# Another order in the opening of a two-layer decoder trunk, transposes where float32 blocks were multiplied with the identity, and casts of the sums of h put in turn with the attention's

## The chip, the cores and the metric

The kernel runs on one core of one Trainium2 chip. The metric is device microseconds of one execution. A core has TensorE (PE in the profile; its weight loads are PEld), VectorE (DVE), ScalarE (ACT), GpSimd (POOL) and SyncE (SP), whose queue issues the DMAs.

## The reference

Two layers, each a token mixer and a gated convolutional FFN, on x of 1024 tokens by 1024 features, all in float32:

```python
for l in range(DEPTH):                       # 2
    h = rmsnorm(x, norm1[l])
    proj = h @ w_in[l]                       # 1024 x 5120: q/k/v of both mixers, two gates
    qa, ka, va, qb, kb, vb, gate_pre = jnp.split(proj, splits, axis=-1)
    o_a = dilated_mixture(...)               # 3 groups of 4 heads, windows 128/512/2048, dilations 1/4/16
    o_b = stick_breaking_attention(...)      # 4 heads
    gates = jax.nn.sigmoid(gate_pre + b_gate[l])
    merged = g_a * (o_a @ w_br[l, :OUT_A]) + g_b * (o_b @ w_br[l, OUT_A:])
    x = x + merged @ w_o[l]
    up = rmsnorm(x, norm2[l]) @ w_up[l]      # 1024 x 5632
    a, v = up[..., :D_FF], up[..., D_FF:]
    a = causal_depthwise_conv(a, conv_w[l], conv_b[l])
    x = x + (jax.nn.gelu(a, approximate=False) * v) @ w_down[l]
return rmsnorm(x, norm_f)
```

## The kernel before

Activations lie with features on the partitions and tokens along the free axis, in two halves of 512 tokens (`n` = 0, 1). Every large operand of a product is kept in two parts: `split` (L124) has ScalarE cast the source to a high part (line L125) and VectorE subtract it for the low part (L126). A product is then three matmuls: high by high, high by low, low by high (`product`, L147; lines L151 to L153). Small products that need full float32, such as a product with the identity matrix `ident`, are issued as one float32 matmul.

TensorE's order is the order of the program text (`manual_schedule`). The orders of ScalarE, VectorE, GpSimd and of SyncE's queue are made by the compiler's scheduler from dependencies, priorities and modelled costs, and are fixed when the program runs: an instruction that waits holds up what stands behind it on its engine. Buffers are allocated from pools by tag; an allocation waits until a buffer of its tag is free (tag `e8` has 6, `xa` 4, `p4` 4, `ql` 2, `wh` and `wl` 4 each; PSUM has two banks for each of the tags `ps`, `s`, `t` and `o`).

**The opening.** `first` (L1761) brings x in, 128 tokens (a chunk) at a time: DMA of 512 KB, square and root on ScalarE (L1778, L1779), a reciprocal (L1780) and two multiplications with the gain (L1783) on VectorE, eight transposes (L1786, tile `x_t`) on TensorE, and a two-part cast into H (tiles `hh` and `hl`). `mixer` (L1114) issues the attention's masks (`masks`, L79), starts the small loads of `setup` (L1792), and then lets `drive` alternate: one chunk of `first`, two steps of `head` (L559). `head` loads and casts the weights for the stick-breaking mixer's values, keys and queries, and computes the values of one chunk (`values_part`, L494, two steps of 12 matmuls each, tile `v_ps`), then keys and queries.

**The attention and what runs beside it.** `attend` (L307) goes through a list of items: stick-breaking (B..), near window (N.., `p0` tiles) and dilated windows (T.., `p1` tiles). Between two operations of an item it advances the dense work by a rate, some matmuls of the gates, further projections and so on. An item transposes its weights to PSUM, `parts` (L583) casts them in two (tiles `p0h`, `p0l`) with high priority, and `apply` multiplies them with the values (L709). Each call of `advance` first calls `aside` (L224), which takes one step from a list of side work. The list begins with `block_sums` (L889): four sums of blocks of H for the products that are done with seven block products instead of eight (`seven`). The first two series of sums (numbers 3 and 1) take three GpSimd subtractions or additions for each of four blocks (L900 to L902, tile `h_sum`), and then `in_two` (L914) casts each in two (tiles `t_hi`, `t_lo`). In `series` (L920) a sum begins every `gap` = 5 steps, and its cast comes `lag` = 4 steps after it. Series 3 begins after item B17, series 1 after the scores of N01.

**Products with the identity.** `join` (L852) ends a pair of heads: it spreads 16 blocks of factors (`fx`, 128x128) by multiplying them with `ident` (L860, tile `j_ps`), into two banks of `t` and two of `o`; the bank of `o` that is used last is released by `fold` (L596), which takes the attention's last output out of it. `norm` (L455) spreads the reciprocal roots of four blocks of tokens in the same way (L470, tile `nrm_b`). `join` runs four times, `norm` six.

**The residual.** Near the end of layer 0's mixer `residual_in` (L1100) loads x again, a chunk at a time, turns it (tile `x_t`, L1111), and ScalarE copies it to the residual stream X (L1112).

## Time and profile before

| | |
|---|---|
| median of 3 runs | 2724.53 us (2723.65 to 2727.9) |
| the profiled execution | 2726.66 us |
| its span in the trace | 2724.8 us |
| instructions | 36820 |
| TensorE busy | 2678.4 us, 98% of the span |
| VectorE, ScalarE, GpSimd busy | 74%, 50%, 25% |
| mean granted clock of TensorE | 0.996 |
| DMA | 420.52 MB, mean 154 GB/s |

The span is the time from the first to the last recorded instruction; the execution's time lies a little over it. A row of a timeline gives the start, the duration, engine, line, operation, tiles written and read, how many instructions are merged in it, and in brackets how long the engine had stood idle before it and what ended that. In a row of a stretch the numbers after the length are busy us (and instructions) of PE, PEld, DVE, ACT and POOL, then TensorE's granted clock, the DMA engines' busy share and GB/s. A matmul's recorded duration overlaps the next one's; the distance of two starts is what it costs.

### The profile page before, as it was taken

What the parts mean: (1) busy time and instruction counts of PE and PEld (TensorE: products, weight loads), DVE (VectorE), ACT (ScalarE), POOL (GpSimd) and SP (SyncE); (2) the same over time, 40 slices, a digit from 0 to 9 for tenths busy, and PEclk for the clock granted to TensorE, in tenths of its full rate; (3) what the DMA queues carried; (4) which work ended last, traced back from release to release, by engine and by line L of the source; (5) the groups of instructions that cost most, each with busy time, mean ns of one, the idle gap of its engine ahead of it and who ended that gap; (6) DMA issues with size and microseconds to landing.
All of it is one profiled execution on the core that took longest, in us unless ns stands there. A gap on an engine that the chain in (4) does not pass through costs nothing.

```text
span 2724.8 us, 36820 instructions
## 1 busy us (share of the span) xinstructions
PE 2678.4 (98%) x13194; PEld 2249.0 (83%) x13194; DVE 2018.9 (74%) x2976; ACT 1352.2 (50%) x2494; POOL 669.0 (25%) x485
## 2 busy tenths in 40 slices
PE   8999999999999999999999999999999999999999
PEld 8987888888888888888888878888788888888888
DVE  5776766675789888897657767565848888998865
ACT  5655545465455555432335556454645455554225
POOL 1004211122124433321110051211212343443210
PEclk9999999999999999999999999999999999999999
DMA  5112268564334444688411122784722444446863
GB/s 152 34 53 69 60 173 260 176 225 130 89 116 164 139 161 139 216 325 315 165 36 42 48 82 61 198 257 162 257 87 81 141 152 149 170 139 245 330 252 123
DMA packets 356738, 420.52 MB, mean 154 GB/s; under 512 B 20700, under 2 KB 285260, under 8 KB 355020
## 3 DMA queue, kind: packets, MB, share of 16 engines
q1 hardware_dynamic: 356556, 418.18, 46.4%
q8 instruction: 104, 1.70, 0.3%
q14 instruction: 78, 0.64, 0.1%
HBM read 278.59 MB, written 139.53 MB: 153 GB/s over the span
## 4 chain that ended last, share of the span: by engine, by line
PE 83%; DVE 9%; issue 2%; ACT 2%; POOL 2%; DMA 1%; SPq 0%; DVEq 0%; ACTq 0%; POOLq 0%
PE u_a L883 5%; PE u_a L885 5%; PE u_a L884 5%; PE d_ps L1585 4%; PE d_ps L1586 4%; PE d_ps L1587 4%; PE u_c L885 3%; PE u_c L883 3%; PE u_c L884 3%; PE i_a L883 2%; PE i_a L884 2%; PE i_a L885 2%; PE o_ps L151 2%; PE o_ps L152 2%; PE o_ps L153 2%
## 5 line engine op out<-in xcount | busy, mean ns | idle before, releaser
L126 DVE TENSOR_TENSOR w_lo<-up_a,w_hi 128x512 fp32r<-128x512 f32 x240 | 237.4, 996 | 21.9 <-ACT w_hi L125 21.9
L125 ACT CAST w_hi<-up_a 128x512 fp32r<-128x512 f32 x240 | 149.4, 622 | 185.2 <-PE u_a L884 43.2
L1593 DVE TENSOR_TENSOR x<-x,d_ps 128x512 f32<-128x512 f32 (+1 forms) x228 | 151.8, 671 | 78.1 <-PE d_ps L1587 76.6
L1324 POOL TENSOR_TENSOR cv<-cv 128x512 f32<-128x512 f32 x88 | 132.3, 1516 | 249.3 <-DVE cv L1319 139.5
L126 DVE TENSOR_TENSOR w_lo<-w_raw,w_hi 128x512 fp32r<-128x512 f32 x152 | 112.6, 743 | 60.7 <-ACT w_hi L125 60.3
L126 DVE TENSOR_TENSOR g<-cv,g 128x512 fp32r<-128x512 f32 x154 | 152.5, 991 | 5.2 <-ACT g L125 2.7
L125 ACT CAST w_hi<-w_raw 128x512 fp32r<-128x512 f32 x152 | 94.2, 620 | 114.9 <-PE o_ps L152 71.2
L126 DVE TENSOR_TENSOR w_lo<-in_a,w_hi 128x512 fp32r<-128x512 f32 x120 | 87.9, 734 | 67.5 <-ACT w_hi L125 66.9
L125 ACT CAST w_hi<-in_a 128x512 fp32r<-128x512 f32 x120 | 74.5, 621 | 122.2 <-PE i_c L884 49.4
L1585 PE MATMUL d_ps<-gd_in,w_hi 128*128 128x512 f32 (+1 forms) x340 | 130.3, 383 | 1.7 <-issue 0.8
L1587 PE MATMUL d_ps<-gd_in,w_lo 128*128 128x512 f32 (+1 forms) x340 | 129.8, 382 | 0.0
L1586 PE MATMUL d_ps<-gd_in,w_hi 128*128 128x512 f32 (+1 forms) x340 | 129.8, 382 | 0.0
L883 PE MATMUL u_a<-hh,w_hi 128*128 128x512 f32 x320 | 124.6, 390 | 2.1 <-DVE u L1475 2.1
L884 PE MATMUL u_a<-t_lo,w_hi 128*128 128x512 f32 x320 | 124.5, 389 | 0.0
L883 PE MATMUL u_a<-t_hi,w_hi 128*128 128x512 f32 x320 | 124.5, 389 | 0.0
L884 PE MATMUL u_a<-hl,w_hi 128*128 128x512 f32 x320 | 124.5, 389 | 0.0
L885 PE MATMUL u_a<-hh,w_lo 128*128 128x512 f32 x320 | 124.5, 389 | 0.0
L885 PE MATMUL u_a<-t_hi,w_lo 128*128 128x512 f32 x320 | 124.5, 389 | 0.0
L623 DVE TENSOR_TENSOR_SCAN stay<-stay,zero 128x128 f32<-128x128 f32 (+3 forms) x64 | 86.9, 1357 | 42.7 <-ACT stay L621 42.5
L1585 PE MATMUL d_ps<-gd_in,wd 128*128 128x512 f32 (+1 forms) x292 | 113.9, 390 | 0.0
L125 ACT CAST g<-cv 128x512 fp32r<-128x512 f32 x154 | 94.9, 616 | 37.5 <-POOL cv L1324 29.8
L1587 PE MATMUL d_ps<-gd_in,wd 128*128 128x512 f32 (+1 forms) x292 | 112.8, 386 | 0.0
(398 smaller groups left out, 8659.0 us busy)
## 6 DMA issues: line engine op xcount, KB each, us to landing
gd<-g SPq DMA_DIRECT2D x154, 512.0 KB, 3.4
gd_in<-gd SPq DMA_DIRECT2D x154, 512.0 KB, 6.4
up_a<-in_w_up_dram SPq DMA_DIRECT2D x80, 512.0 KB, 5.6
t_kq<-tk SPq DMA_DIRECT2D x32, 768.0 KB, 4.9
wd_raw<-in_w_down_dram SPq DMA_DIRECT2D x22, 1024.0 KB, 8.5
w_raw<-in_w_in_dram SPq DMA_DIRECT2D x80, 256.0 KB, 3.1
in_a<-in_w_in_dram SPq DMA_DIRECT2D x40, 512.0 KB, 4.6
gin<-gs SPq DMA_DIRECT2D x32, 512.0 KB, 4.7
```

Source lines behind the costliest of these rows:

```text
L125: act.copy(hi, src)
L126: dve.tensor_tensor(lo, src, f32(hi), ALU.subtract)
L151: pe.matmul(o, lh, rh, start=(first and i == 0), stop=False, skip_group_check=share)
L623: dve.tensor_tensor_scan(rev, rev, zero[:, 0:1].to_broadcast([P, L]), 1.0, ALU.mult, ALU.add)
L883: pe.matmul(o, w[0][:, c], rh, start=(first and i == 0), stop=False, skip_group_check=True)
L884: pe.matmul(o, w[0][:, c], rl, start=False, stop=False, skip_group_check=True)
L885: pe.matmul(o, w[1][:, c], rh, start=False, stop=(last and i == 3), skip_group_check=True)
L1324: return lambda: pool.tensor_tensor(dst, a, b, ALU.subtract)
L1585: pe.matmul(o[:, sub], wh[:, c], gh[:, sub], start=(i == 0 and k in (0, 4, 5)), stop=False, skip_group_check=True)
L1586: pe.matmul(o[:, sub], wh[:, c], gl[:, sub], start=False, stop=False, skip_group_check=True)
L1587: pe.matmul(o[:, sub], wl[:, c], gh[:, sub], start=False, stop=(i == m - 1), skip_group_check=True)
L1593: dve.tensor_tensor(x, x, o[:, sub], ALU.add)
```

## The change

1. The opening is written out in another order. x's first chunk is also transposed as it came (`kept`), stored to DRAM later and reloaded into X, so that `residual_in` leaves that chunk out. The value weights are loaded and cast by `first` itself, two of their four low parts on GpSimd; their loads stand behind those of x's first two chunks. One warming matmul less is issued. The squares go to tag `e8` instead of `ql`. Casts of chunk i follow the scaling of chunk i+1. `mixer` issues the first three chunks with ScalarE and VectorE in the order of the text: a chunk, one step of values, a chunk, one step, the masks, a chunk, two steps. The loads of key and query weights and of `setup` come later.
2. `norm` and `join` use a transpose in place of the float32 matmul with `ident`.
3. In `block_sums` the GpSimd operations are chained one sum after the other; a sum's ScalarE cast is ordered after the last attention cast that was issued before it (an ordering alone, no wait); the gap is 4 steps instead of 5, and the lag 6 instead of 4.

```diff
--- before.py
+++ after.py
@@ -31,10 +31,11 @@
 GRP = 2
 NRAW = 2
 PT = 6
-WARM = 6
+WARM = 5
 GROUPS = (2, 2, 3, 4)
 READY = 6
 ET = mybir.EngineType
+NO_SYNC = mybir.DependencyInfo(mybir.DependencyClass.NoSync, mybir.DependencyReason.DATA)
 IN_ORDER = {ET.PE, ET.Activation, ET.DVE, ET.Pool}
 HEAD = 4
 SECOND = 0.35
@@ -121,8 +122,16 @@
     def quarter(name, dtype=F32, c=HF):
         return sb.tile([P, 2048 // c, c], dtype, tag="xa", bufs=4, name=name)
 
-    def split(hi, lo, src):
-        act.copy(hi, src)
+    LAST = {}
+
+    def split(hi, lo, src, turn=None):
+
+
+        one = act.copy(hi, src)
+        if turn == "is":
+            LAST["act"] = one.ins.name
+        elif turn == "waits" and LAST:
+            tc.add_manual_dep(one.ins, LAST["act"], NO_SYNC, reason="in turn")
         dve.tensor_tensor(lo, src, f32(hi), ALU.subtract)
 
 
@@ -467,7 +476,7 @@
         yield
         rb = bank(tag, "nrm_b")
         for c in range(4):
-            pe.matmul(rb[:, c * P : (c + 1) * P], ss[:, 4 + c : 5 + c].to_broadcast([P, P]), ident, start=True, stop=True, skip_group_check=True)
+            pe.transpose(rb[:, c * P : (c + 1) * P], ss[:, 4 + c : 5 + c].to_broadcast([P, P]), ident)
         yield
         new_h(n)
         for e in range(KD):
@@ -563,13 +572,20 @@
             x = [big(name, F32R) for _ in range(n)] if l else None
             return x and ([x[0][:, h, :] for h in range(2)] if n == 1 else [y.rearrange("p a b -> p (a b)") for y in x])
 
-        wv = weights(w_in[l][:, OFF_VB : OFF_VB + 256], 256, place(2, "v_w"))
-        wk, wq = (weights(w_in[l][:, off : off + P], P, place(1, "kq_w")) for off in (OFF_KB, OFF_QB))
+        wv = weights(w_in[l][:, OFF_VB : OFF_VB + 256], 256, place(2, "v_w")) if l else early.pop("wv")
+        others = lambda: [weights(w_in[l][:, off : off + P], P, place(1, "kq_w")) for off in (OFF_KB, OFF_QB)]
+        if l:
+            wk, wq = others()
         yield
         vt = R["vb"] = new_v("vb")
         kt = R["kb", 0] = big("kt", F32R)
         q = R["qb", 0] = new_q()
-        yield from values_part(vt, wv, range(2 if l else 4))
+        if l:
+            yield from values_part(vt, wv, range(2))
+        else:
+            yield from values_part(vt, wv, range(1))
+            wk, wq = others()
+            yield from values_part(vt, wv, range(1, 4))
         for n in range(2):
             yield from keys_half(kt, wk, n)
             yield from queries_half(q, wq, n, SCALE)
@@ -584,7 +600,7 @@
 
         hi, lo = small(name + "h", F32R), small(name + "l", F32R)
         with tc.high_priority(offset=AHEAD):
-            split(hi[:, :n], lo[:, :n], src[:, :n])
+            split(hi[:, :n], lo[:, :n], src[:, :n], "is")
         return hi, lo
 
     def fold(dst, o):
@@ -857,7 +873,7 @@
             for a in range(2):
                 o = bank("to"[n], "j_ps")
                 for r in range(4):
-                    pe.matmul(o[:, r * P : (r + 1) * P], fx[a][:, n, r, :], ident, start=True, stop=True, skip_group_check=True)
+                    pe.transpose(o[:, r * P : (r + 1) * P], fx[a][:, n, r, :], ident)
                 spread.append(o.rearrange("p (r j) -> p r j", r=4))
         mine = on[:, pr, :].rearrange("p (n j r) -> p n r j", n=2, r=4)
         other = ot.rearrange("p (r n j) -> p n r j", r=4, n=2)
@@ -897,9 +913,11 @@
                     keep["r"] = quarter("h_sum")
                 new_s(t)
             r, (ah, al), (bh, bl) = keep["r"][:, i, :], a()[i], b()[i]
-            pool.tensor_tensor(r, f32(al), f32(bl), ALU.subtract)
+            one = pool.tensor_tensor(r, f32(al), f32(bl), ALU.subtract)
+            if "last" in keep:
+                tc.add_manual_dep(one.ins, keep["last"], NO_SYNC, reason="one sum after the other")
             pool.tensor_tensor(r, r, f32(ah), ALU.add)
-            pool.tensor_tensor(r, r, f32(bh), ALU.subtract)
+            keep["last"] = pool.tensor_tensor(r, r, f32(bh), ALU.subtract).ins.name
 
         def further(t, a, i):
             if t == 4:
@@ -912,7 +930,7 @@
             dve.tensor_tensor(r, r, f32(al), ALU.add)
 
         def in_two(t, i):
-            split(*S[t][i], keep["r"][:, i, :])
+            split(*S[t][i], keep["r"][:, i, :], "waits")
 
         b11, b12, b21, b22 = (lambda n=n, k=k: half(n, k) for k in range(2) for n in (1, 0))
         todo = []
@@ -926,8 +944,8 @@
             for k in range(3 * gap + lag + 1):
                 todo.append((after, lambda fs=at.get(k, ()): [g() for g in fs]))
 
-        series({"B17"}, 3, lambda i: first(3, b22, b12, i), 4, 5)
-        series({"N01s"}, 1, lambda i: first(1, b12, b11, i), 4, 5)
+        series({"B17"}, 3, lambda i: first(3, b22, b12, i), 6, 4)
+        series({"N01s"}, 1, lambda i: first(1, b12, b11, i), 6, 4)
         series({"N11s"}, 2, lambda i: further(2, b22, i), 1, 1)
         series({"plain"}, 4, lambda i: further(4, b21, i), 1, 1)
         return todo
@@ -1100,7 +1118,7 @@
     def residual_in():
 
         for n in range(2):
-            for c in range(4):
+            for c in range(0 if n else 1, 4):
                 xr = sb.tile([P, T], F32, tag="ql", bufs=2, name="xr")
                 t0 = n * HF + c * P
                 nc.sync.dma_start(xr, xin[t0 : t0 + P, :])
@@ -1113,12 +1131,29 @@
 
     def mixer(l, pending):
         R.clear()
-        if l == 0:
-            masks()
         vectors = setup(l)
-        next(vectors)
-        first_units = relay(heads.pop(l)[0], primed=True) if l else relay(head(l))
-        drive(pending, first_units, 2.0 if l == 0 else 0.7, 0 if l == 0 else HEAD)
+        if l:
+            next(vectors)
+            drive(pending, relay(heads.pop(l)[0], primed=True), 0.7, HEAD)
+        else:
+            first_units = relay(head(l))
+
+            with tc.manual_schedule(engines={ET.Activation, ET.DVE}):
+                next(pending)
+                next(first_units)
+                for n in (1, 2):
+                    next(pending)
+                    for _ in range(n):
+                        next(first_units)
+                    if n == 1:
+                        masks()
+            for i, _ in enumerate(pending):
+                for _ in range(2):
+                    next(first_units, None)
+                if i == 1:
+                    next(vectors)
+            for _ in first_units:
+                pass
         for _ in vectors:
             pass
         dense = Dense()
@@ -1210,6 +1245,8 @@
         if l == 0:
             for n in range(2):
                 new_x(n)
+            for h in range(2):
+                nc.sync.dma_start(X[0][h][:, :, 0:P], xs[0][:, 4 * h : 4 * h + 4, 0:P])
         next(wo[0])
         next(residual, None)
 
@@ -1660,7 +1697,7 @@
             pass
         return box[0]
 
-    heads = {}
+    heads, early = {}, {}
 
     def enter(l):
 
@@ -1762,32 +1799,85 @@
         gb = sb.tile([P, T], F32, tag="ot", name="gb")
         warm = sb.tile([P, 8], F32, tag="ss", bufs=2, name="warm")
         act.activation(warm[:, 0:1], eps, AF.Sqrt)
+        xr, rest, tps = {}, {}, {}
+        raw = big("w_raw").rearrange("p a (b c) -> p (a b) c", c=256)
+        wv = early["wv"] = []
+
+        def load(i):
+            if i < 8:
+                xr[i] = sb.tile([P, T], F32, tag="p4", bufs=4, name="xr")
+                nc.sync.dma_start(xr[i], xin[i * P : (i + 1) * P, :])
+
+        def weights_in(r):
+            nc.sync.dma_start(raw[:, r : r + 2, :], w_in[0].rearrange("(k p) n -> p k n", p=P)[:, r : r + 2, OFF_VB : OFF_VB + 256])
+
+        def weights_split(r, eng):
+            hi = sb.tile([P, 2, 256], F32R, tag="wh", bufs=4, name="w_hi")
+            lo = sb.tile([P, 2, 256], F32R, tag="wl", bufs=4, name="w_lo")
+            act.copy(hi, raw[:, r : r + 2, :])
+            eng.tensor_tensor(lo, raw[:, r : r + 2, :], f32(hi), ALU.subtract)
+            wv.extend((hi[:, i, :], lo[:, i, :]) for i in range(2))
+
+        def turned(src, tag):
+            got = [bank(tag, "x_t") for _ in range(2)]
+            for k in range(KD):
+                pe.transpose(got[k // 4][:, (k % 4) * P : (k % 4 + 1) * P], src[:, k * P : (k + 1) * P], ident)
+            return [tp.rearrange("p (e t) -> p e t", e=4) for tp in got]
+
+        def scaled(i):
+            sq = rest[i] = big("xsq")[:, 0, :]
+            ss = sb.tile([P, 8], F32, tag="ss", bufs=2, name="ss")
+            act.activation(sq, xr[i], AF.Square, accum_out=ss[:, 0:1])
+            act.activation(ss[:, 1:2], ss[:, 0:1], AF.Sqrt, bias=eps[:, 0:1], scale=1.0 / D)
+            dve.reciprocal(ss[:, 2:3], ss[:, 1:2])
+            yield
+            for h in range(2):
+                hd = slice(h * HF, (h + 1) * HF)
+                dve.scalar_tensor_tensor(sq[:, hd], xr[i][:, hd], ss[:, 2:3], gb[:, hd], ALU.mult, ALU.mult)
+            yield
+
+        def in_two(i):
+            n, c = i // 4, i % 4
+            if c == 0:
+                new_h(n)
+            for h in range(2):
+                split(*(y[:, 4 * h : 4 * h + 4, c * P : (c + 1) * P] for y in H[n]), tps[i][h])
+
+        load(0)
+        nc.sync.dma_start(gb, norm1[0].partition_broadcast(P))
+        load(1)
+        for r in range(0, KD, 2):
+            weights_in(r)
+        load(2)
         wp = bank("t", "warm")
         for _ in range(WARM):
             pe.matmul(wp[:, 0:P], ident, ident, start=True, stop=True)
-        for n in range(2):
-            new_h(n)
-            for c in range(4):
-                t0 = n * HF + c * P
-                xr = sb.tile([P, T], F32, tag="p4", bufs=4, name="xr")
-                nc.sync.dma_start(xr, xin[t0 : t0 + P, :])
-                if n == 0 and c == 0:
-                    nc.sync.dma_start(gb, norm1[0].partition_broadcast(P))
-                sq = sb.tile([P, T], F32, tag="ql", bufs=2, name="xsq")
-                ss = sb.tile([P, 8], F32, tag="ss", bufs=2, name="ss")
-                act.activation(sq, xr, AF.Square, accum_out=ss[:, 0:1])
-                act.activation(ss[:, 1:2], ss[:, 0:1], AF.Sqrt, bias=eps[:, 0:1], scale=1.0 / D)
-                dve.reciprocal(ss[:, 2:3], ss[:, 1:2])
-                for e0 in (0, 4):
-                    hd = slice(e0 * P, (e0 + 4) * P)
-                    dve.scalar_tensor_tensor(xr[:, hd], xr[:, hd], ss[:, 2:3], gb[:, hd], ALU.mult, ALU.mult)
-                    tp = bank("s", "x_t")
-                    for e in range(4):
-                        pe.transpose(tp[:, e * P : (e + 1) * P], xr[:, (e0 + e) * P : (e0 + e + 1) * P], ident)
-                    tv = tp.rearrange("p (e t) -> p e t", e=4)
-                    hi, lo = (h[:, e0 : e0 + 4, c * P : (c + 1) * P] for h in H[n])
-                    split(hi, lo, tv)
-                yield
+        f = [scaled(i) for i in range(8)]
+        next(f[0])
+        kept = turned(xr[0], "t")
+        next(f[0])
+        tps[0] = turned(rest[0], "s")
+        next(f[1])
+        weights_split(0, dve)
+        in_two(0)
+        weights_split(2, pool)
+        next(f[1])
+        weights_split(4, dve)
+        weights_split(6, pool)
+        yield
+        for i in range(1, 8):
+            tps[i] = turned(rest[i], "s")
+            if i < 7:
+                for _ in f[i + 1]:
+                    pass
+            in_two(i)
+            load(i + 2)
+            if i == 5:
+                part = quarter("x_part", F32, P)
+                for h in range(2):
+                    act.copy(part[:, 4 * h : 4 * h + 4, :], kept[h])
+                nc.sync.dma_start(xs[0][:, :, 0:P], part[:, 0:KD, :])
+            yield
 
     def setup(l):
 
@@ -1809,7 +1899,6 @@
 
     with tc.manual_schedule(engines={mybir.EngineType.PE}):
         pending = first()
-        next(pending)
         for l in range(depth):
             pending = mixer(l, pending)
             pending = ffn(l, pending, enter(l + 1) if l + 1 < depth else leave)
```

## The prediction

> **What bounds the kernel now.** I read the page first, then the waits of TensorE, then its busy time in 5 us stretches, and last the timelines around the places the change touches.
>
> ```profile
> span 2724.8 us, 36820 instructions
> PE 2678.4 (98%) x13194; PEld 2249.0 (83%) x13194; DVE 2018.9 (74%) x2976; ACT 1352.2 (50%) x2494; POOL 669.0 (25%) x485
> PEclk9999999999999999999999999999999999999999
> ```
>
> TensorE is busy 2678.4 of 2724.8 us, so only two things can shorten the program: fewer instructions on TensorE, or fewer of the 46.4 us in which it idles (with the slow stretches that follow an idle time). The profiled execution took 2726.66 us, 1.86 more than its span; the median of the runs is 2724.53, which is 2.13 less. I add up against 2726.66 and subtract 2.13 at the end. A measurement of this kernel can tell about 0.2% from no change, 5.4 us.
>
> The waits of TensorE name one of the places that the change aims at (columns: total us, times, longest):
>
> ```profile
> PE o L709 <- DVE p0l L126: 5.9, 6, 2.0
> PE o L709 <- ACT p0h L125: 4.5, 6, 1.5
> ```
>
> These are the window attention's products, which wait for the two-part cast of their transposed weights: 10.4 us in all, the largest pair in the list.
>
> **The sums of h.** ScalarE, VectorE, GpSimd and TensorE around the worst of these waits, in layer 0:
>
> ```profile
> 245.45 2.55 POOL L900 TENSOR_TENSOR h_sum<-hl 128x512 f32<-128x512 f32 x2 [13.66 <-PE sb_o L645]
> 250.97 2.53 POOL L902 TENSOR_TENSOR h_sum<-h_sum,hh 128x512 f32<-128x512 f32 x2
> 260.65 0.62 ACT L125 CAST t_hi<-h_sum 128x512 fp32r<-128x512 f32 x1 [5.14 <-POOL h_sum L902]
> 262.95 0.48 ACT L125 CAST p0h<-t 128x384 fp32r<-128x384 f32 x1
> 261.30 2.79 DVE L126 TENSOR_TENSOR t_lo<-h_sum,t_hi 128x512 fp32r<-128x512 f32 x2 [4.95 <-ACT t_hi L125]
> 263.48 0.39 PE L709 MATMUL o<-p0h,v 128*128 128x256 f32 x1 [1.50 <-ACT p0h L125]
> 265.88 0.58 PE L709 MATMUL o<-p0l,v 128*128 128x256 f32 x1 [2.01 <-DVE p0l L126]
> ```
>
> ScalarE stands 5.14 us at the cast of a sum that GpSimd hasn't finished, and the cast p0h that TensorE needs is queued behind it. GpSimd works two sums abreast (x2 in its rows), so the first is complete only at 253.5, 8 us after its start. What this costs, by stretches (second column TensorE busy, then its instructions; the clock is the seventh number after the stretch, the share ahead of DMA):
>
> ```profile
> 255.00:260.00 5.00, 4.17 (x21) 3.31 (x21) 1.35 (x2) 0.51 (x2) 5.00 (x5) 1.00 0.02 3
> 260.00:265.00 5.00, 2.36 (x12) 1.48 (x10) 3.50 (x6) 2.09 (x4) 5.00 (x4) 1.00 0.00 0
> 265.00:270.00 5.00, 4.12 (x15) 3.52 (x16) 3.36 (x11) 4.91 (x14) 5.00 (x5) 0.66 0.64 262
> 1600.00:1605.00 5.00, 4.25 (x23) 3.17 (x21) 3.27 (x3) 2.60 (x7) 5.00 (x4) 1.00 0.14 42
> 1610.00:1615.00 5.00, 1.47 (x7) 0.85 (x5) 4.80 (x11) 2.80 (x8) 5.00 (x4) 0.90 0.21 90
> 1615.00:1620.00 5.00, 5.00 (x16) 4.13 (x16) 3.36 (x7) 3.35 (x10) 5.00 (x5) 0.50 0.54 198
> 1620.00:1625.00 5.00, 5.00 (x27) 4.16 (x26) 2.04 (x7) 2.35 (x7) 5.00 (x5) 0.91 0.97 280
> ```
>
> Layer 0 idles 0.83 + 2.64 + 0.88 = 4.35 and then works 4.12 us at 0.66, which loses 1.40. Layer 1 idles 0.75 + 3.53 = 4.28 and loses 0.15 + 2.50 + 0.45 = 3.10 to the clock. Together 13.1 us. No single wait in the layer 0 rows is longer than 2.01 us, and the clock fell all the same. The Trainium skill ("TensorE: Matmul & The Clock Gate", why this matters for your kernels) warns of idle gaps over about 3 us; by that alone the clock would not fall in layer 0 and taking the waits away would save no clock there. The rows decide, so I count the clock.
>
> The change has three parts here. Each sum on GpSimd is chained behind the one before, so the first is complete after three operations of 1.3 to 1.7 us, about 4 us. The cast is placed 6 steps after its sum instead of 4. And it comes after the last cast of the attention issued so far on ScalarE. A step is an attention operation plus some six products of TensorE, 1.4 to 1.9 us, so six are about 10 us: twice the 4 us that GpSimd needs. The casts should no longer stand in ScalarE's queue waiting, and what they hold up, p0h and the exponentials, is free. What is late next is VectorE:
>
> ```profile
> L126 DVE TENSOR_TENSOR t_lo<-h_sum,t_hi x24: 677/1112/1785, 252.9 to 1678.1; 128x512 fp32r<-128x512 f32 x24
> ```
>
> The low part of a sum takes 0.68 us at best and 1.40 each in the row at 261.30, with GpSimd at work. Four per layer fall into the window attention; each can put up to about 0.65 us ahead of a p0l. All four doing so would take 2.6 per layer; I take half, 1.3. **Sums: 13.1 - 2.6 = 10.5 us saved, bounds 4 to 13.1.**
>
> **The products with the identity.** A float32 product of 128x128 is two instructions on TensorE; the same as a transpose is one, as the x_t rows further down show.
>
> ```profile
> 498.61 3.79 PE L860 MATMUL j_ps<-ident,fx 128*128 128x128 f32 x32
> 502.15 0.47 PE L883 MATMUL i_a<-hh,w_hi 128*128 128x512 f32 x1
> 499.43 0.68 DVE L596 TENSOR_TENSOR ot<-o,fold 64x512 f32<-64x512 f32 x1 [1.26 <-ACT fold L595]
> 572.34 3.95 PE L860 MATMUL j_ps<-ident,fx 128*128 128x128 f32 x32
> 574.39 0.69 DVE L596 TENSOR_TENSOR ot<-o,fold 64x512 f32<-64x512 f32 x1
> 1924.45 1.16 PE L860 MATMUL j_ps<-ident,fx 128*128 128x128 f32 x8 [0.16 <-DVE ot L596]
> 695.69 1.05 PE L470 MATMUL nrm_b<-ident,ss 128*128 128x128 f32 x8
> 696.50 0.48 PE L151 MATMUL o_ps<-hh,w_hi 128*128 128x512 f32 x1
> ```
>
> A join spreads 16 blocks in 32 instructions, 3.54 us from 498.61 to the next product. Sixteen transposes at 0.10 are 1.6, so four joins could save 4 x 1.94 = 7.8. They won't save all: the last four blocks go to the buffer of PSUM that the fold at L596 releases. In the first join the fold ends at 500.11, after the first twelve (498.61 + 1.2), so the last four run to about 500.55: 1.6 saved. In the second the fold ends at 575.08 and the block ends at 575.5 instead of 576.0: 0.5. I take the first join of layer 1 like that of layer 0, 1.6. In the last (the 1924.45 row) the fold was just awaited already; it stands behind a multiplication that reads the first blocks and so moves up by half of their time: 1.0. **Joins 4.7 us, bounds 3 to 7.8**: the lower end is both late folds giving nothing.
>
> The norm's block of 8 takes 0.81 us to the next product, 4 transposes 0.40. Six norms: **2.4 us, bounds 1 to 2.5**. TensorE is full around them, and the multiplications that read nrm_b start earlier too.
>
> **The opening.**
>
> ```profile
> 4.39 1.06 ACT L1778 ACTIVATE xsq<-xr 128x1024 f32<-128x1024 f32 x1 [2.15 <-DMA xr<-in_x_dram]
> 7.53 1.06 ACT L1778 ACTIVATE xsq<-xr 128x1024 f32<-128x1024 f32 x1 [1.66 <-DMA xr<-in_x_dram]
> 6.10 1.41 DVE L1783 SCALAR_TENSOR_TENSOR xr<-xr,ss,gb 128x512 f32<-128x512 f32 x2
> 7.43 0.26 DVE L84 CAST mask_b<-msk 128x128 bf16<-128x128 f32 x1
> 8.82 0.42 DVE L94 TENSOR_TENSOR base<-msk,msk 128x256 bf16<-128x256 f32 x1
> 6.91 1.97 PE L1786 MATMUL x_t<-ident,xr 128*128 128x128 f32 x8 [2.40 <-DVE xr L1783]
> 12.57 1.94 PE L1786 MATMUL x_t<-ident,xr 128*128 128x128 f32 x8 [3.69 <-issue]
> 14.16 0.56 PE L151 MATMUL v_ps<-w_hi,hh 128*128 128x256 f32 x1
> 18.38 1.04 PE L1786 MATMUL x_t<-ident,xr 128*128 128x128 f32 x8
> 19.17 0.36 PE L151 MATMUL v_ps<-w_hi,hh 128*128 128x256 f32 x1
> 22.91 0.36 PE L151 MATMUL v_ps<-w_hi,hh 128*128 128x256 f32 x1
> ```
>
> From 14.16 on TensorE is full, one chunk of 128 tokens each 3.74 us (19.17 to 22.91). So only what happens before it counts: how early the first product starts, and whether VectorE then keeps up. Eight raw transposes now fill the idle time between 4.39 and 6.91 (1.97 at the slow pace): free. The first chunk is scaled by 7.5 and turned by 8.9 as before. Its two-part cast (two casts, two subtractions, about 2 us) ends near 11, and the first half of the first value product can run before chunk 1 is turned, where it waited for 14.16. I expect it to finish near 13.2, because its second pair of weight rows gets its low part on GpSimd (1.3 to 1.7). Chunk 1's transposes follow, then the second half, to about 16. But VectorE, now in written order, does the masks (7.43 to 9.24, 1.8 us) after chunk 1's split instead of in its idle time; chunk 2's scaling (1.41) and split wait behind them. So the products of chunk 1 start about 17.3 instead of 19.17, and those of chunk 2 about 21.6 instead of 22.91. Per chunk VectorE has some 3 us of work against 3.74, so nothing more is lost. **Opening 1.3 us saved**; bounds 3 saved (VectorE never late) and 1 lost (weights landing late: five small loads leave the path of the queue, but 1 MB of weights now stands ahead of chunk 2).
>
> The Trainium skill ("TensorE: Matmul & The Clock Gate", PE-mode transpose) says that transposes don't count as busy for the clock gate. By that rule the eight new ones and one warming product less leave TensorE at the slow pace (8 in 1.97 against 8 in 1.04) for longer. Worked out from rows: twelve products at 0.24 instead of 0.12 lose 1.4, and the opening saves nothing. The rows can't separate it, since transposes and products were mixed when the pace rose; it is a rival below.
>
> In the stage that adds the residual, eight transposes go: 0.79 us (18.38 to 19.17). Two reloads of 256 KB stand in the DMA queue instead of one load of 512 KB, each waiting for its buffer; if the gate loads queued behind them are held up, 1 us is lost. **0.8 saved, bounds -1 to 0.9.** The other moved steps (k and q weights, setup's small loads, the store of the kept part) are issued while TensorE has a queue of products; their cover is those products, and uncovered a load costs its few us once.
>
> **Sum.** 10.5 + 4.7 + 2.4 + 1.3 + 0.8 = 19.7 us. 2726.66 - 19.7 = 2706.96, less 2.13: **2704.8 us**.
>
> **The rivals.**
> First, the waits move to VectorE: ScalarE is freed, but t_lo and the sums' neighbours delay p0l, and only 5 of the 13.1 us come back. The 1.40 us of t_lo under GpSimd speak for it; against it, p0l is issued with high priority and t_lo now follows p0h. 19.7 - 5.5 = 14.2 saved: 2710.3. Chance 0.20.
> Second, the clock rule of transposes holds: 18.3 saved, 2706.2. Chance 0.12.
> Third, TensorE's saved time returns as waits (the joins' on the fold, the norms' on VectorE) and the sums' waits only shift: about 4 us saved, 2720. The 98% speak against it. Chance 0.05.
> Fourth, slower: the low parts of all eight GpSimd sums per layer land ahead of a p0l with their longest 1.78 us. That is 28.5 us, and a slow spell of 3.1 per layer besides: 34.7 lost against 13.1 + 9.2 saved, so 2737. It decides from the point where they cost over 22.3 us, 1.4 each. TensorE then idles in the window attention more than before. Chance 0.05.
> The forecast has 0.58.
>
> **How the numbers follow.** The best ends add up to 27.3 saved (2697.2); the worst ends, with the first rival, to about 7 (2717.5). I give 2697 to 2717; beyond it lie the third and fourth rival and a little of the rest. Faster by over 5.4 us: forecast and first two rivals, 0.90; within: 0.05; slower: 0.05.
>
> **What would show it.** Right: 64 instructions on the join's line and 24 on the norm's; no ScalarE wait of several us at t_hi, and clock 1.00 where it was 0.66 and 0.50; the waits for p0h and p0l under 4 us in all; first value product before 12, that of chunk 2 near 21.6. Wrong: transposes at more than 0.15 us apart, new idle of TensorE at the first products that read t_hi or in the window attention, or a join's block still ending where it did.

## The result, and the profile after

| | before | changed |
|---|---|---|
| median, us (runs beside each other) | 2726.22 (2723.65 to 2727.93, 4 runs) | 2706.47 (2704.98 to 2709.53, 4 runs) |
| profiled execution, us | 2726.66 | 2705.66 |
| its span, us | 2724.8 | 2703.6 |

The changed kernel takes 0.993 of the time before (95% interval 0.9918 to 0.9943): 19.75 us less, where 19.7 were forecast. In a second set of runs, beside the kernel before, it saved 19.8 (0.9926, 0.9913 to 0.9938). That the total came out so closely is luck: three of its terms were missed, the sums by 6.5 us one way, the joins and the opening by 2.4 and 1.7 the other way.

The page of the changed kernel, the same lines as of before:

```profile
span 2703.6 us, 36629 instructions
PE 2663.9 (99%) x13104; PEld 2236.2 (83%) x13104; DVE 2012.4 (74%) x2974; ACT 1351.8 (50%) x2494; POOL 673.2 (25%) x487
```

The span is 21.2 us shorter, TensorE's busy time 14.5. The 90 instructions fewer are the forecast ones: 64 in the joins, 24 in the norms, one float32 product (two instructions) in the warming. At 0.10 each they are some 9 us of the busy time; most of the rest is products that were slow or stood alone before, as the stretches below show.

TensorE's waits in the changed kernel (total us, times, longest):

```profile
PE sb_o L661 <- DVE sbl L135: 5.1, 2, 2.7
PE j_ps L876 <- DVE ot L612: 4.8, 4, 1.7
PE o L725 <- DVE p0l L135: 2.2, 2, 1.1
```

The window attention's products wait 2.2 us for p0l instead of 5.9, and p0h, 4.5 before, is gone from the list. New in second place are the joins, which wait for the fold four times.

**The sums of h**, the timeline of layer 0:

```profile
245.68 1.30 POOL L916 TENSOR_TENSOR h_sum<-hl 128x512 f32<-128x512 f32 x1 [13.68 <-PE sb_o L661]
248.53 1.62 POOL L920 TENSOR_TENSOR h_sum<-h_sum,hh 128x512 f32<-128x512 f32 x1
259.78 0.47 ACT L130 CAST p0h<-t 128x384 fp32r<-128x384 f32 x1
260.15 0.62 ACT L130 CAST t_hi<-h_sum 128x512 fp32r<-128x512 f32 x1
261.22 0.55 DVE L135 TENSOR_TENSOR p0l<-t,p0h 128x384 fp32r<-128x384 f32 x1
261.69 1.32 DVE L135 TENSOR_TENSOR t_lo<-h_sum,t_hi 128x512 fp32r<-128x512 f32 x1
```

The first sum is complete at 250.15 and is cast ten us later, behind p0h, with no wait in brackets. On VectorE too the low part of the sum comes after p0l. The same work in five-microsecond stretches, in layer 1 some 11 us earlier than before (after the length TensorE's busy time comes first, and its clock stands ahead of the DMA share):

```profile
260.00:265.00 5.00, 5.00 (x30) 4.28 (x29) 5.00 (x6) 2.56 (x5) 4.21 (x4) 1.00 0.23 65
265.00:270.00 5.00, 5.00 (x28) 4.19 (x27) 2.78 (x8) 2.35 (x7) 3.67 (x3) 1.00 1.01 291
1605.00:1610.00 5.00, 5.00 (x28) 4.19 (x27) 2.15 (x4) 2.44 (x5) 3.66 (x4) 1.00 0.64 183
```

TensorE idles nowhere in them, and the clock is 1.00 where it was 0.66 and 0.50. What this is worth is read from the time that the same work takes, from the first sum to the end of the window attention, in each layer; first the kernel before, then the changed one:

```profile
245.00:340.00 95.00, 88.35 (x458) 73.20 (x457) 66.60 (x133) 53.36 (x129) 41.14 (x29) 0.98 0.21 67
1594.00:1690.00 96.00, 89.41 (x455) 73.97 (x454) 66.20 (x131) 53.32 (x129) 40.70 (x29) 0.96 0.21 67
```

```profile
245.00:332.00 87.00, 85.40 (x460) 72.29 (x459) 64.10 (x134) 53.11 (x129) 40.33 (x29) 1.00 0.24 74
1583.00:1670.00 87.00, 85.47 (x460) 72.28 (x459) 64.10 (x134) 53.20 (x129) 39.89 (x29) 1.00 0.24 74
```

About 460 products took 95 and 96 us and take 87: 8 + 9 = 17 us, not the 10.5 of the forecast.

**The products with the identity**, the timeline of the changed kernel at the first join and the first norm:

```profile
491.53 1.50 PE L876 MATMUL j_ps<-ident,fx 128*128 128x128 f32 x12
492.19 1.09 DVE L883 TENSOR_TENSOR on<-on,j_ps 128x512 f32<-128x512 f32 x1 [1.11 <-PE j_ps L876]
493.31 0.68 DVE L612 TENSOR_TENSOR ot<-o,fold 64x512 f32<-64x512 f32 x1
494.05 0.66 PE L876 MATMUL j_ps<-ident,fx 128*128 128x128 f32 x4 [1.02 <-DVE ot L612]
494.46 0.48 PE L899 MATMUL i_a<-hh,w_hi 128*128 128x512 f32 x1
...
686.61 0.60 PE L479 MATMUL nrm_b<-ident,ss 128*128 128x128 f32 x4
686.96 0.48 PE L160 MATMUL o_ps<-hh,w_hi 128*128 128x512 f32 x1
```

A transpose costs 0.10 as forecast (12 in about 1.3 us), but the last four stand 1.02 us for the fold at L612, which VectorE took up only after the multiplication at L883. The block lasts 2.93 us to the next product; 3.54 before. The four blocks together: 14.74 before, 12.43 now, 2.3 saved. A norm's block takes 0.35 where it took 0.81, and the other norms are like it.

**The opening** of the changed kernel:

```profile
2.49 2.50 PE L1854 MATMUL warm<-ident 128*128 128x128 f32 x10 [2.49 <-POOL ident masks.py:199]
10.31 0.58 PE L160 MATMUL v_ps<-w_hi,hh 128*128 128x256 f32 x1 [1.61 <-ACT hh L130]
11.34 2.98 POOL L1818 TENSOR_TENSOR w_lo<-w_raw,w_hi 128x512 fp32r<-128x512 f32 x2 [4.30 <-ACT w_hi L1817]
11.61 3.26 DVE L1836 SCALAR_TENSOR_TENSOR xsq<-xr,ss,gb 128x512 f32<-128x512 f32 x2
13.92 2.17 PE L1824 MATMUL x_t<-ident,xsq 128*128 128x128 f32 x8
18.66 0.36 PE L160 MATMUL v_ps<-w_hi,hh 128*128 128x256 f32 x1
22.42 1.16 PE L1824 MATMUL x_t<-ident,xsq 128*128 128x128 f32 x8 [0.64 <-DVE hl L135]
23.34 0.36 PE L160 MATMUL v_ps<-w_hi,hh 128*128 128x256 f32 x1
44.14 0.40 PE L160 MATMUL k_ps<-hh,w_hi 128*128 128x512 f32 x1
```

The first product starts at 10.31 instead of 14.16 as forecast. But chunk 1's products start at 18.66 (forecast 17.3) and chunk 2's at 23.34 (forecast 21.6, before 22.91), and the first product of the keys comes 0.4 us later than in the kernel before: of the 3.85 us won at the start nothing is left. Some 1.8 of them were no gain to begin with: chunk 1's eight transposes stood ahead of the first product before and stand behind it now (13.92 to 15.75). VectorE's scaling of the second chunk took 3.26 us beside GpSimd's subtraction, where the forecast had 1.41.

### The profile page after: what moved, and what is told of

It is laid out like the page before. It is cut to its first block, busy times and chain, and to the rows that moved or that the text cites. A ratio compares the mean times of both kernels' runs of the same rounds, so it can differ in the third digit from the quotient of the medians.

```text
span 2703.6 us, 36629 instructions
## 1 busy us (share of the span) xinstructions
PE 2663.9 (99%) x13104; PEld 2236.2 (83%) x13104; DVE 2012.4 (74%) x2974; ACT 1351.8 (50%) x2494; POOL 673.2 (25%) x487
## 4 chain that ended last, share of the span: by engine, by line
PE 82%; DVE 10%; issue 2%; ACT 2%; DMA 1%; POOL 1%; SPq 0%; DVEq 0%; POOLq 0%; ACTq 0%
PE u_a L899 5%; PE u_a L901 5%; PE u_a L900 5%; PE d_ps L1622 4%; PE d_ps L1624 4%; PE d_ps L1623 4%; PE u_c L901 3%; PE u_c L899 3%; PE u_c L900 3%; PE o_ps L160 2%; PE o_ps L162 2%; PE o_ps L161 2%; PE i_a L899 2%; PE i_a L900 2%; PE i_a L901 2%
```

## The experiments

**1. The sums' part alone.** The kernel before, with the chain, the order and the steps:

```diff
-            split(hi[:, :n], lo[:, :n], src[:, :n])
+            split(hi[:, :n], lo[:, :n], src[:, :n], "is")
-            split(*S[t][i], keep["r"][:, i, :])
+            split(*S[t][i], keep["r"][:, i, :], "waits")
-        series({"B17"}, 3, lambda i: first(3, b22, b12, i), 4, 5)
+        series({"B17"}, 3, lambda i: first(3, b22, b12, i), 6, 4)
```

and the same for the series N01s, with the chain on GpSimd.

> The kernel before with the third part of the change alone (sums chained, casts in turn, 6 steps and 4). Theory A: the waits for casts behind GpSimd's sums were worth more than the 13.1 us that the prediction counted, and they sit wholly in this part: 16 to 18 us faster than before, stretch 245 to 340 about 8 us shorter, 1594 to 1690 about 9. Theory B: the part gives the 10.5 us of the forecast and the rest of what the changed kernel shows in those stretches comes from the other parts' shift of the schedule: 9 to 12 us faster.

Measured: 2707.52 us, 0.9933 of before (0.9921 to 0.9946): 18.9 less by the medians, 17.0 by the spans, as theory A had it. The sums are nearly all of the change.

**2. The transposes alone.** The kernel before, with `pe.transpose` in `norm` and `join`:

```diff
-                    pe.matmul(o[:, r * P : (r + 1) * P], fx[a][:, n, r, :], ident, start=True, stop=True, skip_group_check=True)
+                    pe.transpose(o[:, r * P : (r + 1) * P], fx[a][:, n, r, :], ident)
```

> The kernel before with transposes in norm and join alone. Theory A: a join's block ends when VectorE has added the fold, and VectorE now multiplies first, so joins give 2 to 2.5 us in all instead of 4.7, norms about 2: 3.5 to 5 us faster. Theory B: the forecast's order of VectorE holds without the rest of the change: joins 4.7, norms 2.4, 6 to 7.5 us faster.

Measured: 2725.54, 0.9995 (0.9986 to 1.0004); the span is 2.3 us shorter. This is less than either theory, and by the whole time not to be told from no change. The waits of this kernel show where the joins' part went:

```profile
PE j_ps L860 <- DVE ot L596: 4.8, 4, 1.7
```

It is the same wait, to the tenth, as in the changed kernel: shortening the block turned it into a wait for the fold. Counted by their blocks, joins and norms save 5.0 us here (2.3 and 2.7), which is more than the whole time allows (at most 3.8). In the profile some 2 us go at one place of layer 1: TensorE waits 1.44 us for `st` near 1815 in both kernels, with granted clock 1.00 after it before the change and 0.66 here (1.7 us), and a new wait of 0.31 stands ahead of it. Whether that is chance or comes with the shifted order is not shown.

**3. The opening alone.** The changed kernel without its sums' part and its transposes in `norm` and `join`, so the new opening and the residual stage remain:

```diff
-                    pe.transpose(o[:, r * P : (r + 1) * P], fx[a][:, n, r, :], ident)
+                    pe.matmul(o[:, r * P : (r + 1) * P], fx[a][:, n, r, :], ident, start=True, stop=True, skip_group_check=True)
-            split(*S[t][i], keep["r"][:, i, :], "waits")
+            split(*S[t][i], keep["r"][:, i, :])
...
```

> The kernel before with the new opening and the residual's first chunk kept. Theory A (trace of the changed kernel): keys begin 0.4 us later than before, the residual stage is 0.8 us shorter: between 1 us faster and 0.5 us slower. Theory B (forecast): opening 1.3 and residual 0.8: 2 us faster, first key product near 42.4.

Measured: 2725.47, 0.9997 (0.9988 to 1.0006). The opening brings nothing that can be measured, as its theory A had it.

**4. Without the order on ScalarE.** The changed kernel; the sum's cast no longer comes after the attention's casts, chain and steps stay:

```diff
-            split(*S[t][i], keep["r"][:, i, :], "waits")
+            split(*S[t][i], keep["r"][:, i, :])
```

> The changed kernel without the order of the casts after the attention's casts; the chain on GpSimd and the 6 and 4 steps stay. Theory A: the order is what counts; the scheduler again puts the casts of sums ahead where it believes GpSimd done, and 5 us or more of waits for p0h and p0l return. Theory B: the chain counts, since a sum is complete after 4 us instead of 8: within 2 us of the changed kernel.

Measured: 2723.56, 0.9991 (0.9982 to 1.0). Of the change 2.9 us are left by the medians. Its timeline, the same place:

```profile
254.71 0.63 ACT L130 CAST t_hi<-h_sum 128x512 fp32r<-128x512 f32 x1 [3.70 <-POOL h_sum L920]
258.96 0.62 ACT L130 CAST t_hi<-h_sum 128x512 fp32r<-128x512 f32 x1 [2.74 <-POOL h_sum L920]
259.49 0.58 ACT L130 CAST p0h<-t 128x512 fp32r<-128x512 f32 x1
260.12 0.58 PE L725 MATMUL o<-p0h,v 128*128 128x256 f32 x1 [4.46 <-ACT p0h L130]
```

and its stretches there:

```profile
255.00:260.00 5.00, 0.65 (x3) 0.19 (x1) 1.49 (x2) 2.26 (x7) 4.84 (x4) 0.94 0.00 0
260.00:265.00 5.00, 4.22 (x12) 3.35 (x13) 2.41 (x4) 1.53 (x4) 4.77 (x5) 0.50 0.01 3
```

The compiler's scheduler puts two t_hi ahead of this p0h. ScalarE stands 3.70 and 2.74 us for GpSimd, p0h is queued behind, and TensorE stands 4.46 us. Waits of ScalarE at t_hi for h_sum add up to 23.2 us, eight in all (21.5 before the change); in the changed kernel, and in the two that follow, there are none.

**5. The old steps.** The changed kernel with the cast 4 steps behind its sum, one sum each 5 steps:

```diff
-        series({"B17"}, 3, lambda i: first(3, b22, b12, i), 6, 4)
+        series({"B17"}, 3, lambda i: first(3, b22, b12, i), 4, 5)
```

and the same for N01s.

> The changed kernel with the old 4 steps from a sum to its cast and 5 from sum to sum; order and chain stay. Theory A: the order after the attention's casts does the work, and 4 steps (some 7 us) still exceed the 4 us of a chained sum: within 2 us of the changed kernel. Theory B: the distance in steps matters by itself: 4 us or more slower than the changed kernel, with waits of ScalarE at t_hi again.

Measured: 2704.3, 0.9928 (0.9912 to 0.9945). The whole saving is there without the new steps.

**6. Without the chain on GpSimd.**

```diff
-            if "last" in keep:
-                tc.add_manual_dep(one.ins, keep["last"], NO_SYNC, reason="one sum after the other")
```

> The changed kernel without the chain of the sums on GpSimd; order and steps stay. Theory A: the cast comes so late that even two sums worked abreast (8 us) are done: within 2 us of the changed kernel. Theory B: the first casts wait for GpSimd again, some 3 us per layer and a slow spell: 6 us or more slower.

Measured: 2702.99, 0.9924 (0.9909 to 0.9938). Its timeline has the two sums abreast again:

```profile
248.32 3.06 POOL L917 TENSOR_TENSOR h_sum<-h_sum,hh 128x512 f32<-128x512 f32 x2
251.35 2.52 POOL L918 TENSOR_TENSOR h_sum<-h_sum,hh 128x512 f32<-128x512 f32 x2
```

The first sum is thus complete only at about 252.6 (half of the second row's 2.52 after 251.35), 2.5 us later, and nobody waits for it. With runs 4 and 5: without the order the gain is gone, though chain and steps stand; with the order, leaving out either the chain or the steps makes no difference that can be told. The order without both of them was not run.

**7. The fold first.** The changed kernel, with the join's first two multiplications ordered on VectorE after the fold's addition:

```diff
-            dve.tensor_tensor(dst, o[0:64, :], tmp[0:64, :n], ALU.add)
+            LAST["fold"] = dve.tensor_tensor(dst, o[0:64, :], tmp[0:64, :n], ALU.add).ins.name
...
+            for x in (one, two):
+                tc.add_manual_dep(x.ins, LAST["fold"], NO_SYNC, reason="after the fold")
```

> The changed kernel with the join's first multiplications on VectorE ordered after the addition of the fold (an ordering alone). Theory A: what holds the last four transposes of a join is VectorE's order; they come about 0.9 us earlier in each of four joins: waits of TensorE for the fold 1.5 us in all instead of 4.8, some 3 us faster than the changed kernel. Theory B: the later multiplications delay what the branch products read, and TensorE waits there instead: under 1 us.

Measured: 2703.01, 0.9925 (0.991 to 0.994). The first join in its timeline:

```profile
489.50 2.21 PE L876 MATMUL j_ps<-ident,fx 128*128 128x128 f32 x16
490.31 0.68 DVE L612 TENSOR_TENSOR ot<-o,fold 64x512 f32<-64x512 f32 x1 [1.27 <-ACT fold L611]
491.03 1.10 DVE L883 TENSOR_TENSOR on<-on,j_ps 128x512 f32<-128x512 f32 x1
```

The fold now ends at 490.99 and the sixteen transposes run through. The block lasts 1.96 us instead of 2.93; the four together 9.55, 5.2 less than before the change, and the waits for the fold fall from 4.8 to 1.8. That VectorE's order held up the joins is shown; by the whole time alone these 2.9 us can't be told from the changed kernel's.

**8. The raw transposes as products.** The changed kernel, with the first eight as float32 products:

```diff
-                pe.transpose(got[k // 4][:, (k % 4) * P : (k % 4 + 1) * P], src[:, k * P : (k + 1) * P], ident)
+                if plain:
+                    pe.matmul(there, one, ident, start=True, stop=True, skip_group_check=True)
+                else:
+                    pe.transpose(there, one, ident)
...
-        kept = turned(xr[0], "t")
+        kept = turned(xr[0], "t", True)
```

> The changed kernel with the eight transposes of the raw first chunk issued as float32 products with the identity (16 instructions). If transposes do not count as busy for the clock, the pace of TensorE now rises earlier: the first value products at 0.12 us apart from about 12 on, keys begin 1 us earlier. If they count the same, the pace still rises near 16 and keys begin within 0.4 us of the changed kernel, or later because the longer block pushes chunk 0's transposes.

Measured (one run): 2705.23. TensorE was at the fast pace from 7.6 us on: chunk 0's eight transposes took 1.07, and the products behind them stood 0.12 apart, where in the changed kernel they stood 0.21 or more apart until 13.71. Even so the keys' first product starts at 43.95, only 0.2 earlier than in the changed kernel, where a fast pace was expected to give 1 us. TensorE waits for VectorE instead, the longest time at

```profile
15.07 0.63 PE L1828 MATMUL x_t<-ident,xsq 128*128 128x128 f32 x4 [1.02 <-DVE xsq L1840]
```

So the pace is not what holds the opening up; VectorE is. The other profiles say the same: in the seven that have this opening (the changed kernel twice, runs 3 to 7) the last product of chunk 0 starts anywhere from 16.90 to 17.84, by the pace, and the keys start at 43.99 to 44.26 all the same. The three profiles with the old opening have 43.70 to 44.02. The rival of the clock rule is neither shown nor excluded: the pace went as the rule says, in one run, but it differs by itself. In five of those seven profiles chunk 0's transposes took 1.23 us and in two 1.94, with nothing but the warming and eight transposes ahead of them. The clock column does not help here: it reads 1.00 in run 8, and also before the change, where products stood 0.21 apart from 14.52 to 16.44.

**9. The masks early.** The changed kernel, with VectorE's masks in its idle time after chunk 0's scaling:

```diff
         next(f[0])
+        masks()
         tps[0] = turned(rest[0], "s")
...
-                    if n == 1:
-                        masks()
```

> The changed kernel with the masks issued right after chunk 0's scaling, in VectorE's idle time, instead of after chunk 1's split. Theory A: VectorE sets the opening and the masks' 1.8 us stand in its way: the transposes of chunk 3 start about 1.2 us earlier (21.2 instead of 22.4) and keys 0.5 to 1.2 us earlier. Theory B: TensorE's slow pace sets it: keys begin within 0.3 us of the changed kernel.

Measured (one run): 2702.25. The keys start at 43.54, 0.6 earlier than in the changed kernel and outside the spread of its profiles, and the wait ahead of chunk 3's transposes is gone. They start at 21.96, though, not at the 21.2 of theory A, as TensorE's slow pace lasted to 17.7 in this profile. The scaling beside GpSimd still takes 3.31.

**10. The opening's weights on VectorE.**

```diff
-        weights_split(2, pool)
+        weights_split(2, dve)
...
-        weights_split(6, pool)
+        weights_split(6, dve)
```

> The changed kernel with the low parts of all four pairs of value weights on VectorE, none on GpSimd. Theory A: chunk 1's scaling took 3.26 us instead of 1.41 because GpSimd was at work beside it; now 1.4, and chunk 1's transposes start before 13.9; what VectorE has in addition (1.3) eats most of that, keys within 0.5 us of the changed kernel. Theory B: the long scaling had another cause (the gain's or x's arrival): it stays near 3 us and keys come later.

Measured (one run): 2705.62. Its timeline:

```profile
12.33 1.41 DVE L1836 SCALAR_TENSOR_TENSOR xsq<-xr,ss,gb 128x512 f32<-128x512 f32 x2
21.21 1.42 DVE L1836 SCALAR_TENSOR_TENSOR xsq<-xr,ss,gb 128x512 f32<-128x512 f32 x2
22.55 1.28 DVE L135 TENSOR_TENSOR hl<-x_t,hh 128x512 fp32r<-128x512 f32 x2
23.29 1.25 PE L1824 MATMUL x_t<-ident,xsq 128*128 128x128 f32 x8 [2.03 <-DVE hl L135]
45.11 0.40 PE L160 MATMUL k_ps<-hh,w_hi 128*128 128x512 f32 x1
```

The scaling is back at 1.41: GpSimd beside it was the cause of the 3.26. But the keys start at 45.11, 1.0 later than in the changed kernel, outside what was expected: VectorE is late for chunk 3's transposes by 2.03 us. Weights and masks both stand in its way, and its order differs as well: it scales chunk 4 (21.21) ahead of chunk 2's low part (22.55), on which these transposes wait; in the changed kernel the low part comes first (21.59) and the scaling after it (22.79). That is 1.3 of the 2.03. So this run shows what stretches the scaling, but not what the stretch costs.

**11. All three mends**, runs 7, 9 and 10 together, and **12. the changed kernel again**, on the same chip. The edits are those shown.

> The changed kernel with three edits: masks early, all low parts on VectorE, and the fold's addition first in the joins. If the pieces add up: 2.9 us from the joins and 0.5 to 1.5 from the opening, 3 to 4.5 us faster than the changed kernel on the same chip. If the time returns at the branch products: under 1.5 us.

> The changed kernel itself, beside the version with three edits on the same chip, so that the two can be compared: 19 to 20 us faster than the kernel before.

Measured: 2701.02 (2698.61 to 2702.62, 4 runs), 0.9913 of before (0.9897 to 0.9928), against 2705.51 (2703.3 to 2706.95, 5 runs) of the changed kernel: 4.5 us less, and each of the four runs below each of the five. The timeline of run 11:

```profile
17.02 1.25 PE L1824 MATMUL x_t<-ident,xsq 128*128 128x128 f32 x8 [0.47 <-DVE hl L135]
21.00 1.03 PE L1824 MATMUL x_t<-ident,xsq 128*128 128x128 f32 x8
42.58 0.40 PE L160 MATMUL k_ps<-hh,w_hi 128*128 128x512 f32 x1
```

Chunk 3 waits for nothing and the keys start 1.6 us earlier than in the changed kernel, 1.1 earlier than before the change: the opening now gives nearly what it was forecast to give (1.3). Beside run 9, which has the weights on GpSimd, the keys come 1.0 earlier, but in this profile the slow pace ended near 14.9 and in run 9 at 17.7, so how much of that belongs to the weights is not shown. With VectorE's delays gone, the pace counts. This is the fastest version measured here.

## Why the prediction was right, and where it was not

- **Sums, forecast 10.5, measured 17** (8 + 9 by the stretches, 17.0 by the span of run 1). The place and the stall were right; the term was mis-sized, in two ways. Most of the 2.6 taken off for VectorE's low parts did not come: as the rows at 261.22 and 261.69 show, t_lo comes after p0l. Only at the end of the window attention, once per layer, does a p0l that TensorE waits for stand behind t_lo and other low parts: 1.15 us (at 328.61), where it waited 0.85 for p0h and p0l at the same place before. And idle time plus clock undercounts a stall. Summed by the stretches, idle time fell by 5.05 and 5.06 us and the *busy* time of the same products by 2.95 and 3.94. The forecast had 4.35 and 4.28 of idle time, and 1.40 and 3.10 for the clock; later waits of the same stretch shrank as well. That makes 1.5 of idle time, 2.4 of busy time and the 2.6, together the 6.5 us missed. The rest of the busy time is probably the isolated products: one that starts after a wait is recorded with 0.39 to 0.58 us where it costs 0.12 in a row. No run separates that.
- **How the sums gain**: the prediction gave the credit to chain, steps and order together and argued that 6 steps leave twice the time that GpSimd needs. That argument is the step that failed: in run 4 the chain and the 6 steps stand, and ScalarE waits 23.2 us for GpSimd at t_hi all the same, since the scheduler puts the casts ahead. Runs 4, 5 and 6 give the gain to the order. The place in ScalarE's line decided, not the time allowed.
- **Joins, forecast 4.7 (3 to 7.8), measured 2.3 by their blocks.** The step that failed is "the fold ends at 500.11": it took the fold's place from before, where VectorE began it 0.82 us after the join's first product. In the changed kernel the multiplication comes first on VectorE and the fold begins 1.78 us after the first transpose (493.31 less 491.53), so three blocks of four gave 0.6, 0.1 and 0.6, and only the last 1.0. The lower end of 3 left out that the fold itself could move. Run 7 gives 5.2.
- **Norms, forecast 2.4**: 2.7 by the blocks of all six, 0.46 in the one shown. That the whole time falls by as much as the blocks of joins and norms is not shown (run 2).
- **Opening, forecast +1.3 (-1 to 3), measured -0.4**, and by the spread of the profiles (run 8) between -0.6 and 0. The first product came when it was expected. Two steps failed. The first is "then the second half, to about 16": it ran to 17.45, since products and transposes stood at the slow pace for longer than was reckoned. The other is "VectorE has some 3 us of work against 3.74, so nothing more is lost": VectorE had the masks and a scaling that GpSimd's subtractions, put beside it by the change, stretched from 1.41 to 3.26, and TensorE stood behind it until chunk 3's transposes. The other is the one that decided, as the fast pace alone brought 0.2 (run 8). Taking the masks out of the way brought 0.6, together with the warming, which had slipped from 1.58 to 2.49 unforeseen and is back at 1.58 in run 9. What the stretch cost by itself stays open.
- **Residual, forecast 0.8**: eight transposes left the stage. From the first product of br_ps to the first of o_ps it takes 50.7 us in the changed kernel's profile and 51.5 before, so 0.8; over all profiles it is 50.6 to 51.7 with the change and 51.4 to 52.2 without.
- **Adding up**: 17 + 2.3 + 2.7 + 0.8 - 0.4 = 22.4 against 21.2 between the spans. One stall is worse in the changed kernel's profile: TensorE waits 1.99 us for `st` at 458.48, with clock 0.67 in the five microseconds after 460. Before the change the same wait, at 465.60, is 1.43 us long, with 0.72 in the stretch around it. That is 0.6 of idle time and 0.4 of clock, most of the difference; it is a stall that differs from profile to profile (last section).
- **Rivals**: the first (waits move to VectorE) did not come, since p0l's waits fell from 5.9 to 2.2. The second (the clock rule) is open, and the opening brought nothing anyway. The slower one did not come for the same reason as the first: of the 24 low parts on t_lo<-h_sum the median takes 0.69 us, 1.11 before, and the one in the rows shown stands behind p0l. Of the third, the waits for the fold came, for 4.8 us.

## What to carry to other kernels

Where engines work through a fixed order, look first at what stands behind a cast or copy that waits for a slow engine: ordering it after the urgent casts was worth 17 us here without making anything faster. Price a stall by the time that the same products take with and without it, since the busy column counts slow and isolated products as work. After shortening a block, ask anew in what order the engine that feeds its last part will do its work.

## What was not expected of the hardware

The same wait at the same place can cost clock or not. TensorE's wait at L596 for `st`, in the stretch from 455 to 460, is 1.43 us long in run 6 and in run 7. The stretches of run 6, then of run 7:

```profile
455.00:460.00 5.00, 3.57 (x23) 3.06 (x22) 4.46 (x11) 3.13 (x8) 0.52 (x1) 1.00 0.66 156
460.00:465.00 5.00, 5.00 (x30) 4.16 (x29) 1.81 (x4) 2.86 (x7) 2.59 (x2) 1.00 0.83 213
```

```profile
455.00:460.00 5.00, 3.57 (x15) 2.94 (x15) 3.18 (x10) 3.10 (x9) 1.33 (x2) 0.76 0.70 185
460.00:465.00 5.00, 5.00 (x28) 4.19 (x27) 1.81 (x3) 1.97 (x4) 1.22 (x1) 0.90 0.73 192
```

With the same busy time, run 6 did 23 products and kept clock 1.00, in the next stretch too; run 7 did 15 at 0.76, and 0.90 followed. The Trainium skill ("TensorE: Matmul & The Clock Gate", what's actually happening) says that the window in which activity is judged runs freely, and that the point of change depends on where in it the work lands. The two profiles are in keeping with that; no run here shows the window itself. A clock loss of 1 to 2 us read from one profile is therefore not a fixed price.

And VectorE's scaling of two blocks (L1836, two inputs from SBUF) takes 1.41 us alone and 3.26 beside two subtractions of GpSimd. The Trainium skill ("SBUF — State Buffer", two separate sides) has the two engines share a pair of ports, held by one of them for a whole instruction; runs 10 and 11, in which GpSimd is out of the way and the time is 1.41 again, agree.
